# The sample's input projections with the tokens as the stationary operand and the weight panels streaming

## The chip, the cores and the metric

The kernel runs on one core of a Trainium2 chip. The metric is the device time of one execution in microseconds. The core's engines are TensorE (PE in the profile, with its weight loads as PEld), VectorE (DVE), ScalarE (ACT), GpSimd (POOL) and SyncE (SP), whose queue issues the DMAs.

## What is computed

Two layers of a hybrid decoder. A layer normalises its input, multiplies it by one wide matrix `w_in` (1024 x 3920), and gives the slices of the product to four recurrent mixers side by side: retention, HGRN2, GLA and RWKV-7. Their gated outputs go through `w_out`, and a cross-attention to 256 memory tokens follows.

```python
h = rmsnorm(x, norm_mix[l])
p_ret, p_hgrn, p_gla, p_rwkv = split(h @ w_in[l])      # the input projections
o_ret  = retention(rotary(q), rotary(k), v) * silu(g)
o_hgrn = gated_linear(silu(q), (1 - lb) * sigmoid(-f), v=i, log_f) * silu(g)
o_gla  = gated_linear(q, k, v, log_a) * silu(g)
o_rwkv = rwkv7(p + (previous_row - p) * mu) * silu(g)
x = x + concat(o_ret, o_hgrn, o_gla, o_rwkv) @ w_out[l]
x = x + cross_attend(rmsnorm(x, norm_x[l]), memory)
```

This is done for a prompt of 2048 tokens and, with the same weights, for a sample of 8 sequences of 8 tokens each (64 rows), which starts from given states.

## The kernel before

The prompt goes through in four blocks of 512 tokens per layer, so there are eight steps `(l, b)`. The sample's 64 rows ride along: their input projections are made in block 0 of the layer, next to the prompt's, because the weights are there; the four gates' projections for the sample are made in block 1 (`TURN`). The mixers of the sample run as chains of their own: RWKV and GLA in block 0, HGRN and retention in block 1.

Weights come in panels. `load_c` loads a panel of 128 output channels, `load_t` one of 256 in two halves. In block 0 a raw fp32 panel (`wraw`, pool `wrp`, 3 buffers of each) is loaded and `split_w` makes two fp32r parts of it (`whl`, pool `whp`, 3 buffers): the high part by a copy on ScalarE (line 358), the low part by a subtraction on GpSimd. The two parts are stored to DRAM and later blocks load them from there. With `plain` set, `parts_of` gives back the raw panel too, and loads it even where the parts come from DRAM; this is so for the sample's gates in block 1.

The prompt's products use three terms, high x high, high x low and low x high, in fp32r. `dense_c` has the panel's parts stationary and 512 tokens streaming, so channels come out as rows; `dense_t` has 128 tokens stationary and 256 channels streaming, so tokens come out as rows. The sample's products use the raw panel and the raw tokens `hts` (128 x 8 x 64) in plain fp32. `dense_cs` has 64 columns of the panel stationary and the 64 tokens streaming, two halves of the panel into two halves of the PSUM bank. `dense_ts` does the same for a panel of 256 channels, so its result has channels as rows, though the mixer wants tokens as rows: `totok` transposes it later, in the mixer's part of the program (GLA's and HGRN's values, retention's query, key and value).

A layer has 21 column projections for the sample (one of 80 channels for the low-rank inputs, six for RWKV's r, k and v, two for GLA, four for HGRN, eight gates) and 5 row projections.

All these products write PSUM tiles of pool `psd`, which has two banks (`PS("d")`); the mixers' products use the pools `psa`, `psc` and `psb`. A product's bank comes free once it has been read out: for the sample by `shift_mix_s` (RWKV), by copies, by `silu2` (HGRN's query) or in the gates by `evs`.

The order of instructions on each engine is fixed when the program is built, by a list scheduler with priorities: program order, shifted by `PRI` under the name that `rank` gives, and raised for runs of matmuls (`held`). A tile of a tag with one buffer (pool `dnp`, where the projections' results lie) can be written only after the last reader of the tile that had the buffer before. A mixer's working tiles are in pools that are opened one after the other (`wk1` RWKV's prompt part, `wk1s` RWKV's sample, `wk5` GLA's sample, and so on).

Of the kernel before, what the change touches and what calls it, by code (L numbers as in the profile page):

```python
# [142 lines left out]
def decoder(ctx, tc, I, C, O):  # L143
# [270 lines left out]
    def dense_cs(w, hts, ps):  # L414
        raw, hl, M = w
        for k in range(8):
            for h in range(0, M, 64):
                e = min(M, h + 64)
                mm(ps[h:e, :SN], raw[:, k, h:e], hts[:, k, :], k == 0, k == 7)
# [5 lines left out]
    def dense_ts(w, hts, c, ps):  # L425

        for k in range(8):
            for h in (0, 64):
                mm(ps[h:h + 64, :SN], w[k // 4][0][:, k % 4, c * 128 + h:c * 128 + h + 64], hts[:, k, :], k == 0, k == 7)
# [39 lines left out]
    def norm_sample(xt, gcol, hts, wp, xs):  # L469
# [801 lines left out]
    def block(l, b, act, hts, st, smp, on, ons, ds, op):  # L1271
# [15 lines left out]
        wt = load_c([(col("rw_w", 0, 32), 0), (col("rw_a", 0, 32), 32), (col("gla_l", 0, 16), 64)], (l, "low"), smp, not final)  # L1287
# [4 lines left out]
        if smp:  # L1292
            sms = T("sms", [128, SN])
            G.memset(sms[64:128], 0.0)
            ps = PS("d")
            dense_cs(wt, hts, ps)
            shift_mix_s(ps[:80, :SN], 0, c, st["shs"], st["ssh"], sms[:80], 80)
            A.activation(sms[0:32], sms[0:32], AF.Tanh)
        rk = {}
        rks = {}  # L1300
        for j, nm in enumerate("rkv"):
            x = T("dn_" + nm, [128, 2, TB], tag="dn4", bufs=8)
            xs = T("ds_" + nm, [128, 2, SN], tag="ds_" + nm) if smp else None
            for i in range(2):
                wt = load_c([(col("rw_" + nm, i * 128), 0)], (l, "rw", nm, i), smp, not final)
                ps = PS("d")
                dense_c(wt, act, ps)
                shift_mix(ps, 1 + 2 * j + i, c, carry, x[:, i, :])
                if smp:
                    ps = PS("d")  # L1310
                    dense_cs(wt, hts, ps)
                    shift_mix_s(ps[:, :SN], 1 + 2 * j + i, c, st["shs"], st["ssh"], xs[:, i, :])
            rk[nm] = x
            rks[nm] = xs
# [5 lines left out]
        def proj_t(nm, ev, evs):  # L1320
            wt = load_t(col(nm, 0, 256), (l, nm), smp, again=not final)
            for t0 in (0, 2):
                ps = PS("d").rearrange("p (t n) -> p t n", t=2)
                for t in range(2):
                    dense_t(wt, act, t0 + t, ps[:, t, :])
                ev(ps, t0)
            if smp:
                ps = PS("d")
                for i in range(2):
                    dense_ts(wt, hts, i, ps[:, i * SN:])  # L1330
                copy_ps(evs, ps[:, :2 * SN].rearrange("p (c n) -> p c n", c=2))

        def proj_c(nm, o, ev, evs, smp=smp, hts=hts):
            wt = load_c([(col(nm, o), 0)], (l, nm, o), smp, not final)
            ps = PS("d")
            dense_c(wt, act, ps)
            ev(ps)
            if smp:
                ps = PS("d")
                dense_cs(wt, hts, ps)  # L1340
                evs(ps[:, :SN])
# [32 lines left out]
        qks = T("ds_qk", [128, 2, SN]) if smp else None  # L1374
# [4 lines left out]
        gvs = T("ds_gv", [128, 2, SN]) if smp else None  # L1379
# [7 lines left out]
        if b == TURN["gla"]:  # L1387
            with left("wk5") as wp:
                x = ds["gla"]
                R_gla(l, sa, None, dict(x, v=totok(x["v"], 2, sa, wp, "sv", 256)), ons["gla"], wp)  # L1390
        if b == TURN["hgrn"]:
            with left("wk6") as wp:
                x = ds["hgrn"]
                R_hgrn(l, sa, None, dict(x, v=totok(x["v"], 2, sa, wp, "sv", 256)), ons["hgrn"], wp)
        if b == TURN["ret"]:
            with left("wk7") as wp:
                x = {nm: totok(ds["ret"][nm], 2, sa, wp, "sv" + nm, 256) for nm in "qkv"}
# [35 lines left out]
        rqs = {nm: T("ds_r" + nm, [128, 2, SN]) if smp else None for nm in "qkv"}  # L1433
# [360 lines left out]
    def pre_norm(l, b, wp, out, start=False):  # L1794
# [226 lines left out]
```

## Time and profile before

| | us |
|---|---|
| median of 3 runs (lowest to highest) | 3630.43 (3629.65 to 3630.89) |
| the profiled execution | 3625.24 |
| its span | 3623.4 |
| TensorE busy | 3419.7 (94%) |
| TensorE weight loads busy | 2842.5 (78%) |
| VectorE busy | 2283.1 (63%) |
| ScalarE busy | 1393.4 (38%) |
| GpSimd busy | 562.1 (16%) |

Busy time is the time in which at least one instruction of the engine is recorded as running. Matmuls are pipelined, so that records of successive matmuls overlap; what one costs in a stream is read from the distance between starts. A product in plain fp32 leaves two records, one in fp32r leaves one; both are labelled f32. In a tile's name the part before `<-` is what is written, the part behind it the streaming and the stationary operand. The chain of waits is followed back from the last instruction.

### The profile page before, as it was taken

To read this page: it belongs to the slowest core of one execution; us is meant where nothing else is said; L and a number is where in the kernel's file an instruction comes from. 1 tells how busy PE (TensorE), PEld (TensorE's weight loads), DVE (VectorE), ACT (ScalarE), POOL (GpSimd) and SP (SyncE) were. 2 spreads that over 40 slices of the span, in tenths; PEclk is the share of its full clock that TensorE was granted. 3 is DMA by queue.
4 is the path that set the end of the run, shared out by engine and by line. 5 is a ranking of instruction groups with operands and counts; after the bars stand their busy time and mean duration, and the time that the engine had idled before them with its cause. 6 is when DMAs were issued, how large, how long until landed. Compare 5 with 4: busy or idle time off the path is not lost.

```text
span 3623.4 us, 87919 instructions
## 1 busy us (share of the span) xinstructions
PE 3419.7 (94%) x35978; PEld 2842.5 (78%) x35978; DVE 2283.1 (63%) x7543; ACT 1393.4 (38%) x3489; POOL 562.1 (16%) x760
## 2 busy tenths in 40 slices
PE   7899999999999999999999898999989999999998
PEld 5767887778887887788877777778778878877887
DVE  4677645776347754776468765468644577547754
ACT  4443344513235324532445423553214442254323
POOL 3323331020000100110122233101200001000100
PEclk9998999999999999999999989999889999999999
DMA  6432674236652254225442247531555522542254
GB/s 189 150 106 83 214 232 170 72 108 215 210 178 94 92 188 152 105 76 185 164 163 89 98 135 256 176 130 69 151 169 178 180 76 97 200 167 91 72 195 186
DMA packets 244152, 530.87 MB, mean 147 GB/s; under 512 B 66982, under 2 KB 181926, under 8 KB 199718
## 3 DMA queue, kind: packets, MB, share of 16 engines
q1 hardware_dynamic: 243750, 525.25, 42.7%
q8 instruction: 284, 4.65, 0.5%
q14 instruction: 118, 0.97, 0.1%
HBM read 410.04 MB, written 115.16 MB: 145 GB/s over the span
## 4 chain that ended last, share of the span: by engine, by line
PE 73%; DVE 14%; ACT 5%; issue 4%; DMA 2%; POOL 1%; SPq 0%; POOLq 0%; ACTq 0%; DVEq 0%
PE psd L230 39%; PE psc L230 12%; PE psa L230 11%; PE psb L230 5%; PE psc L272 2%; PE psa L272 2%; PE psb L272 2%; DVE rsq L236 1%; DVE Wb L936 1%; DMA wraw<-in_w_in 1%; POOL whl L236 1%; ACT Xb L938 1%; DVE hss L561 1%; DVE sT L745 0%; DVE osb L236 0%
## 5 line engine op out<-in xcount | busy, mean ns | idle before, releaser
L230 PE MATMUL psd<-act,whl 128*128 128x512 f32 (+1 forms) x4032 | 1014.9, 404 | 24.8 <-DVE th L1265 12.9
L230 PEld LDWEIGHTS psd<-act,whl 128*128 128x128 f32 (+1 forms) x4032 | 751.7, 191 | 200.3 <-DVE th L1265 14.7
L230 PE MATMUL psd<-whl,act 128*128 128x256 f32 x3840 | 550.9, 295 | 6.3 <-POOL whl L236 4.6
L230 PEld LDWEIGHTS psd<-whl,act 128*128 128x128 f32 x3840 | 492.3, 196 | 28.6 <-issue 10.3
L236 POOL TENSOR_TENSOR whl<-wraw,whl 128x1024 fp32r<-128x1024 f32 (+1 forms) x90 | 217.7, 2422 | 333.5 <-ACT whl L358 328.5
L230 PE MATMUL psd<-whl,oh 128*128 128x256 f32 x1152 | 211.6, 284 | 2.1 <-DMA whl<-w_w_out 1.5
L280 POOL TENSOR_TENSOR ri<-ri,mhalf 128x1 f32<-128x1 f32 (+1 forms) x87 | 50.0, 575 | 1048.3 <-DVE ri L279 1041.4
L230 PEld LDWEIGHTS psd<-whl,oh 128*128 128x128 f32 x1152 | 177.6, 189 | 3.3 <-DMA whl<-w_w_out 1.7
L230 PE MATMUL psd<-whl,ol 128*128 128x256 f32 x576 | 162.9, 283 | 0.0
L938 ACT ACTIVATE Xb<-X 32x128 f32<-32x128 f32 x324 | 99.1, 306 | 126.1 <-DVE X L954 78.7
L358 ACT ACTIVATE whl<-wraw 128x1024 fp32r<-128x1024 f32 (+1 forms) x90 | 94.1, 1048 | 128.2 <-PE psa L230 40.7
L745 DVE COPY_PREDICATED sT<-upack,psb 128x128 f32<-128x128 uint8 x320 | 92.5, 326 | 41.7 <-PE psb L230 38.2
L236 DVE TENSOR_TENSOR x<-x,psd 128x256 f32<-128x256 f32 x72 | 30.3, 421 | 128.6 <-PE psd L230 128.6
L230 PEld LDWEIGHTS psd<-whl,ol 128*128 128x128 f32 x576 | 108.6, 189 | 0.4 <-DVE ol L236 0.4
L230 PE MATMUL psb<-dn_hq,dn_hf 64*64 64x32 f32 (+1 forms) x3840 | 101.5, 226 | 7.2 <-DVE dn_hq L236 3.2
L230 PEld LDWEIGHTS psb<-dn_hq,dn_hf 64*64 64x64 f32 x3840 | 83.8, 139 | 31.3 <-issue 17.8
L435 ACT ACTIVATE xs<-xn 128x1024 f32<-128x1024 f32 (+1 forms) x34 | 35.9, 1054 | 153.2 <-PE psb L272 150.0
L1265 DVE SCALAR_TENSOR_TENSOR th<-th,psd 128x512 f32<-128x512 f32 x48 | 32.6, 686 | 90.5 <-ACT th L1264 90.4
L230 PE MATMUL psd<-hts,wraw 128*64 128x64 f32 x1984 | 83.9, 229 | 1.9 <-DVE th L1265 1.9
L230 PEld LDWEIGHTS psd<-hts,wraw 128*64 128x64 f32 x1984 | 69.9, 140 | 20.0 <-issue 10.5
L230 PE MATMUL psa<-whl,oh 128*128 128x256 f32 x448 | 82.8, 283 | 0.0
L230 PE MATMUL psc<-whl,oh 128*128 128x256 f32 x448 | 82.7, 283 | 0.0
(760 smaller groups left out, 7361.1 us busy)
## 6 DMA issues: line engine op xcount, KB each, us to landing
whl<-w_w_out SPq DMA_DIRECT2D x56, 1024.0 KB
wraw<-in_w_in SPq DMA_DIRECT2D x76, 512.0 KB
wraw<-in_w_out SPq DMA_DIRECT2D x32, 512.0 KB
w_w_out<-whl SPq DMA_DIRECT2D x16, 1024.0 KB
x<-x SPq DMA_DIRECT2D x32, 512.0 KB
whl<-w_rw_r SPq DMA_DIRECT2D x12, 1024.0 KB
whl<-w_rw_k SPq DMA_DIRECT2D x12, 1024.0 KB
whl<-w_rw_v SPq DMA_DIRECT2D x12, 1024.0 KB
```

Of the source, the lines that this page charges most:

```text
L230: PE.matmul(out, lhsT=lhsT, rhs=rhs, start=start, stop=stop, skip_group_check=True)
L236: e.tensor_tensor(out, a, b, op)
L272: PE.transpose(out, in_, ident[:rows, :rows])
L280: G.tensor_tensor(y, y, mhalf[:P], ALU.pow)
L358: A.activation(hl[:, 0], raw, AF.Copy)
L435: A.activation(out, xt, AF.Square, accum_out=ss[:P])
L561: V.tensor_reduce(ss[:P, :n4], sq[:P, :n4], AX.X, ALU.add)
L745: V.copy_predicated(out, bc(mk, [P, w, 32 // s, s]), ps)
L936: V.tensor_copy(o, i)
L938: A.activation(o, i, AF.Copy)
L1265: V.scalar_tensor_tensor(th, th, 1.0, x, ALU.add, ALU.mult)
```

## The change

For the sample, the normed tokens `hts` become a tile of 128 x 8 x 128 fp32r: the high parts of the 64 tokens beside their low parts. They are the stationary operand, and the panel's two fp32r parts stream past them. A column projection is 16 matmuls (8 slices of the contraction x 2 parts) into a bank with 128 rows, tokens by high and low; ScalarE copies it to SBUF (`scs`, in the buffer of `ths`), and one fp32 matmul against `I64` (two stacked identities) adds the two halves and turns the result into channel rows. A row projection is 16 matmuls of 256 channels, a copy of the upper half and an addition of the lower half, and leaves the tokens as rows, so `totok` is not called for it. No sample projection reads the raw panel any more (`plain` is False). Several of the sample's result tiles share buffers: `ds0` to `ds2` are RWKV's r, k, v and then retention's q, k, v; `ds3` is GLA's value and then HGRN's; `ds4` is GLA's query and key and then HGRN's query.

```diff
-    def dense_cs(w, hts, ps):
-        raw, hl, M = w
-        for k in range(8):
-            for h in range(0, M, 64):
-                e = min(M, h + 64)
-                mm(ps[h:e, :SN], raw[:, k, h:e], hts[:, k, :], k == 0, k == 7)
+    def dense_cs(w, hts):
+
+        _, hl, M = w
+        ps = PS("d")
+        group(ps[:, :M], [(hts[:, k, :], hl[:, j, k, :M]) for k in range(8) for j in range(2)])
+        x = dnp.tile([128, 128], F32, name="scs", tag="ths")
+        A.activation(x[:, :M], ps[:, :M], AF.Copy)
+        ps = PS("d")
+        mm(ps[:M, :SN], x[:, :M], K["I64"])
+        return ps[:M, :SN]
...
-    def dense_ts(w, hts, c, ps):
-
-        for k in range(8):
-            for h in (0, 64):
-                mm(ps[h:h + 64, :SN], w[k // 4][0][:, k % 4, c * 128 + h:c * 128 + h + 64], hts[:, k, :], k == 0, k == 7)
+    def dense_ts(w, hts, out):
+
+        ps = PS("d")[:, :256]
+        group(ps, [(hts[:, k, :], w[k // 4][1][:, j, k % 4, :]) for k in range(8) for j in range(2)])
+        A.activation(out[:SN, 0], ps[:SN], AF.Copy)
+        tt(V, out[:SN, 0], out[:SN, 0], ps[SN:2 * SN], ALU.add)
...
-        tt(V, hts, ps, bc(gcol[:, 0:8].unsqueeze(2), [128, 8, SN]), ALU.mult)
+        x = xs[:, 0:8 * SN].rearrange("p (k n) -> p k n", k=8) if parts else out
+        tt(V, x, ps, bc(gcol[:, 0:8].unsqueeze(2), [128, 8, SN]), ALU.mult)
+        if parts:
+            A.activation(out[:, :, :SN], x, AF.Copy)
+            tt(V, out[:, :, SN:], x, out[:, :, :SN].bitcast(F32), ALU.subtract)
...
-            wt = load_c([(col(nm, o), 0)], (l, nm, o), smp, not final)
+            wt = load_c([(col(nm, o), 0)], (l, nm, o), False, not final)
             ps = PS("d")
             dense_c(wt, act, ps)
             ev(ps)
             if smp:
-                ps = PS("d")
-                dense_cs(wt, hts, ps)
-                evs(ps[:, :SN])
+                evs(dense_cs(wt, hts))
...
-        qks = T("ds_qk", [128, 2, SN]) if smp else None
+        qks = T("ds_qk", [128, 2, SN], tag="ds4") if smp else None
...
-        gvs = T("ds_gv", [128, 2, SN]) if smp else None
+        gvs = T("ds_gv", [128, 1, 256], tag="ds3") if smp else None
...
-                R_gla(l, sa, None, dict(x, v=totok(x["v"], 2, sa, wp, "sv", 256)), ons["gla"], wp)
+                R_gla(l, sa, None, x, ons["gla"], wp)
...
-        hqs = T("ds_hq", [128, 2, SN]) if smp else None
+        hqs = T("ds_hq", [128, 2, SN], tag="ds4") if smp else None
         hfs = T("ds_hf", [128, 2, SN]) if smp else None
-        hvs = T("ds_hv", [128, 2, SN]) if smp else None
+        hvs = T("ds_hv", [128, 1, 256], tag="ds3") if smp else None
...
-        rqs = {nm: T("ds_r" + nm, [128, 2, SN]) if smp else None for nm in "qkv"}
+        rqs = {nm: T("ds_r" + nm, [128, 1, 256], tag="ds%d" % j) if smp else None for j, nm in enumerate("qkv")}
...
-            hts = stp.tile([128, 8, SN], F32, name="hts", tag="hts")
+            hts = stp.tile([128, 8, 2 * SN], F32R, name="hts", tag="hts")
             x = load(xsrc_s(l), SN)
-            norm_sample(x[:SN], cols[l]["g_mix"], hts, wp, scratch())
+            norm_sample(x[:SN], cols[l]["g_mix"], hts, wp, scratch(), True)
```

The RWKV projections, the low-rank ones and HGRN's and retention's mixers are changed in the same way.

## Rows read from the trace of the kernel before

**Rows 1.** The page's first lines: span, and TensorE's busy time.

```profile
span 3623.4 us, 87919 instructions
PE 3419.7 (94%) x35978; PEld 2842.5 (78%) x35978; DVE 2283.1 (63%) x7543; ACT 1393.4 (38%) x3489; POOL 562.1 (16%) x760
```

**Rows 2.** Busy time of the engines, summed over eight stretches with sample projections.

```profile
sum 939.00, PE 855.51 PEld 689.81 DVE 626.07 ACT 364.51 POOL 233.37; mean PE 106.94 PEld 86.23 DVE 78.26 ACT 45.56 POOL 29.17
```

**Rows 3.** TensorE's timeline (start, length, engine, what): sample projections, columns then rows.

```profile
1974.99 1.15 PE L230 MATMUL psd<-hts,wraw 128*64 128x64 f32 x32
1976.07 3.03 PE L230 MATMUL psd<-act,whl 128*128 128x512 f32 x12
...
2151.85 2.08 PE L230 MATMUL psd<-hts,wraw 128*64 128x64 f32 x64
```

**Rows 4.** TensorE's timeline: fp32r runs of 512 and 256 columns, then plain fp32.

```profile
3102.64 11.16 PE L230 MATMUL psd<-act,whl 128*128 128x512 f32 x48
3113.63 0.41 PE L230 MATMUL psd<-whl,oh 128*128 128x256 f32 x2
...
91.39 7.31 PE L230 MATMUL psd<-whl,mh 128*128 128x256 f32 x60 [0.89 <-ACT ds_v L542]
98.53 0.60 PE L272 MATMUL psc<-fpack,wk_xs 128*128 128x128 f32 x4
...
1963.32 0.61 PE L230 MATMUL psc<-vl,w 128*128 128x128 f32 x4
1963.77 0.38 PE L272 MATMUL psa<-fpack,dn_v 128*128 128x128 f32 x2
```

**Rows 5.** Timeline of weight loads, then the products: retention's outputs.

```profile
406.47 0.53 PEld L230 LDWEIGHTS psc<-dn_rv,sT 128*128 128x128 f32 x4
406.92 0.30 PEld L230 LDWEIGHTS psc<-S_ret,rqT 128*128 128x128 f32 x2
...
406.58 0.56 PE L230 MATMUL psc<-dn_rv,sT 128*128 128x64 f32 x4
```

**Rows 6.** Groups by line (busy us, mean ns, idle before): a 128x128 copy from PSUM.

```profile
L944 ACT ACTIVATE XB<-psc 128x128 f32<-128x128 f32 x80 | 22.0, 275 | 15.3 <-PE psc L272 14.3
```

**Rows 7.** Timeline of all engines in the second block's gates, first layer.

```profile
874.82 1.15 PE L230 MATMUL psd<-hts,wraw 128*64 128x64 f32 x32
...
876.35 5.76 PE L230 MATMUL psd<-act,whl 128*128 128x512 f32 x24 [0.38 <-DVE th L1265]
...
877.13 0.63 ACT L1463 ACTIVATE oh<-th 128x512 fp32r<-128x512 f32 x1 [0.89 <-DVE th L1266]
```

**Rows 8.** The chain of waits (start, length): loads of raw panels behind sample projections.

```profile
63.71 6.06 DMA wraw<-in_w_in
...
256.06 4.69 DMA wraw<-in_w_in
...
1896.92 3.94 DMA wraw<-in_w_in
...
1959.91 3.86 DMA wraw<-in_w_in
```

**Rows 9.** VectorE's timeline: HGRN's sample query written, GLA's read last, both layers.

```profile
248.71 0.22 DVE L533 SCALAR_TENSOR_TENSOR ds_hq<-th,psd 128x64 f32<-128x64 f32 x1
...
380.65 0.69 DVE L236 TENSOR_TENSOR qx<-ds_qk,s_bmask 128x512 f32<-128x512 f32 x1
...
1993.33 0.22 DVE L533 SCALAR_TENSOR_TENSOR ds_hq<-th,psd 128x64 f32<-128x64 f32 x1
...
2126.58 0.69 DVE L236 TENSOR_TENSOR qx<-ds_qk,s_bmask 128x512 f32<-128x512 f32 x1
```

**Rows 10.** Groups by line, 258.0 to 381.4 us, then 2005.0 to 2127.3 us.

```profile
L230 PE MATMUL psd<-whl,act 128*128 128x256 f32 x311 | 48.9, 309 | 1.6 <-POOL whl L236 1.3
...
L230 PE MATMUL psd<-whl,act 128*128 128x256 f32 x321 | 48.6, 301 | 3.4 <-POOL whl L236 3.3
```

**Rows 11.** The page's chain that ended last: shares of the span by engine.

```profile
PE 73%; DVE 14%; ACT 5%; issue 4%; DMA 2%; POOL 1%; SPq 0%; POOLq 0%; ACTq 0%; DVEq 0%
```

More of the change, by code (lines that the diff above doesn't have):

```diff
@@ L467, in scaled_tr, with norm_sample @@
                 tt(V, a[:, 1, :, sl], xg, a[:, 0, :, sl].bitcast(F32), ALU.subtract)
-    def norm_sample(xt, gcol, hts, wp, xs):
+    def norm_sample(xt, gcol, out, wp, xs, parts=False):
         norm_rows(xt, SN, wp, xs[:SN])
@@ L1286, in block @@
         G.memset(sm[64:128], 0.0)
-        wt = load_c([(col("rw_w", 0, 32), 0), (col("rw_a", 0, 32), 32), (col("gla_l", 0, 16), 64)], (l, "low"), smp, not final)
+        wt = load_c([(col("rw_w", 0, 32), 0), (col("rw_a", 0, 32), 32), (col("gla_l", 0, 16), 64)], (l, "low"), False, not final)
         ps = PS("d")
@@ L1294, in block @@
             G.memset(sms[64:128], 0.0)
-            ps = PS("d")
-            dense_cs(wt, hts, ps)
-            shift_mix_s(ps[:80, :SN], 0, c, st["shs"], st["ssh"], sms[:80], 80)
+            ps = dense_cs(wt, hts)
+            shift_mix_s(ps, 0, c, st["shs"], st["ssh"], sms[:80], 80)
             A.activation(sms[0:32], sms[0:32], AF.Tanh)
@@ L1302, in block @@
             x = T("dn_" + nm, [128, 2, TB], tag="dn4", bufs=8)
-            xs = T("ds_" + nm, [128, 2, SN], tag="ds_" + nm) if smp else None
+            xs = T("ds_" + nm, [128, 2, SN], tag="ds%d" % j) if smp else None
             for i in range(2):
-                wt = load_c([(col("rw_" + nm, i * 128), 0)], (l, "rw", nm, i), smp, not final)
+                wt = load_c([(col("rw_" + nm, i * 128), 0)], (l, "rw", nm, i), False, not final)
                 ps = PS("d")
@@ L1309, in block @@
                 if smp:
-                    ps = PS("d")
-                    dense_cs(wt, hts, ps)
-                    shift_mix_s(ps[:, :SN], 1 + 2 * j + i, c, st["shs"], st["ssh"], xs[:, i, :])
+                    ps = dense_cs(wt, hts)
+                    shift_mix_s(ps, 1 + 2 * j + i, c, st["shs"], st["ssh"], xs[:, i, :])
             rk[nm] = x
@@ L1320, in proj_t @@
         def proj_t(nm, ev, evs):
-            wt = load_t(col(nm, 0, 256), (l, nm), smp, again=not final)
+            wt = load_t(col(nm, 0, 256), (l, nm), False, again=not final)
             for t0 in (0, 2):
@@ L1327, in proj_t @@
             if smp:
[L1328 to L1331, printed above, removed]
+                dense_ts(wt, hts, evs)
         def proj_c(nm, o, ev, evs, smp=smp, hts=hts):
-            wt = load_c([(col(nm, o), 0)], (l, nm, o), smp, not final)
+            wt = load_c([(col(nm, o), 0)], (l, nm, o), False, not final)
             ps = PS("d")
@@ L1338, in proj_c @@
             if smp:
-                ps = PS("d")
-                dense_cs(wt, hts, ps)
-                evs(ps[:, :SN])
+                evs(dense_cs(wt, hts))
         rank("R_vf")
@@ L1393, in block @@
                 x = ds["hgrn"]
-                R_hgrn(l, sa, None, dict(x, v=totok(x["v"], 2, sa, wp, "sv", 256)), ons["hgrn"], wp)
+                R_hgrn(l, sa, None, x, ons["hgrn"], wp)
         if b == TURN["ret"]:
             with left("wk7") as wp:
-                x = {nm: totok(ds["ret"][nm], 2, sa, wp, "sv" + nm, 256) for nm in "qkv"}
+                x = dict(ds["ret"])
                 tab = sample_const("rots", wp).unsqueeze(1)
```

## The prediction

> **What bounds the kernel now.** I read the page's first section before anything else: TensorE has work in flight for 3419.7 of 3623.4 us, 94% of the span [rows 1]. The next most busy engine, VectorE, has 63%. So a microsecond of TensorE time added or taken away anywhere is, to a first reading, a microsecond of the whole, and the question is where the sample's projections stand. They are in eight stretches: the first block of either layer, and the gates of the second block. The busy time by stretch (the second view) says that TensorE is busy there for 855.5 of 939.0 us, 91% [rows 2]: nearly full, with 83.5 us of gaps. The third view is TensorE's timeline, for what one projection costs. A column projection of the sample (21 in a layer, 42 in all) is 32 records, 16 calls of two records each, and the next instruction starts 1.08 us after its first [rows 3]. A row projection (5 in a layer, 10 in all) is 64 records; with the 0.07 us by which records overlap it holds the engine for 2.01 us [rows 3]. All of them together are 42 x 1.08 + 10 x 2.01 = 65.5 us, 1.8% of the span. That is all that the change could take away on TensorE, if the new form cost nothing.
>
> The profiled execution took 3625.24 us, its span 3623.4; the median of the runs is 3630.43, 0.14% above. I make the sum as a difference and put it on the median.
>
> **What the new form costs on TensorE.** A column projection becomes 16 calls on fp32r operands, which leave one record each: a stationary operand of 128 columns (64 tokens, high parts beside low parts) and 128 moving columns, one panel part each. No row of the trace shows an fp32r product with fewer than 256 moving columns. The bounds: at 512 columns one takes (3113.63 - 3102.64)/48 = 0.229 us, at 256 columns (98.53 - 91.39)/60 = 0.119 us [rows 4]. The slope is 0.110 us for 256 columns, so if the stream alone counted, 128 columns would take 0.119 - 0.055 = 0.064 us: the lower end. But every call loads its stationary operand anew, even where it is that of the call before. The nearest row for a 128-column load with a short stream is the retention output's: stationary 128 columns, 64 moving, and its loads follow each other at (406.92 - 406.47)/4 = 0.112 us [rows 5], though 64 columns stream in at most half of the 0.112 us that 128 take [rows 4]. So I take the load as the pace, between 0.112 and 0.119 us: 0.116. The upper end, if a short fp32r stream ran like a plain fp32 one, is two records of (1963.77 - 1963.32)/4 = 0.112 us [rows 4], 0.225 us a call.
>
> At 0.116 the 16 calls take 1.86 us. Behind them comes the turn back into channel rows, a product of 128 stationary and 64 moving columns in plain fp32: two records at the load's pace, 0.22 us [rows 5]. Together 2.08 us for 1.08: **+1.00 us, x 42 = +42.0 us**. A row projection becomes 16 calls of 256 moving columns: 16 x 0.119 = 1.90 for 2.01, **x 10 = -1.1 us**. The ten turns into token rows (totok) go away, two transposes of 128 columns at 0.112 each [rows 4]: **x 10 = -2.2 us**.
>
> The Trainium skill speaks both for and against this. TensorEngine Tiling, Key Properties, says that a change of the tiling mode drains the engine, and the old form does change it, from 128-column to 64-column tiles and back; such a drain already lies within the 1.08 us measured, so the sum would stay as it is. TensorE: Matmul & The Clock Gate, section Back-to-back issue gap, gives some 81 ns for a load and a product of 128 columns in a steady stream. By it the 16 calls would take 1.30 us, and the 42 projections +18 instead of +42; the fp32 loads of this trace at 0.112 disagree, but no row shows fp32r ones.
>
> **The round trip.** The turn back has to wait for ScalarE to copy the product out of PSUM, 0.28 us by the copy of a 128x128 tile [rows 6]. Where other work for TensorE is at hand this costs nothing. In the second block's gates there is none: dense projections stand one behind the other, and two PSUM banks (pool psd) serve them. There the next dense product starts 876.35 - 874.82 = 1.53 us after the sample's first record [rows 7]. After the change it is 1.86 + 0.55 (the last product in flight, 0.61 - 3 x 0.112 = 0.27 by [rows 4], and the copy) + 0.22 = 2.6 us, +1.1 instead of +1.00; ScalarE can be some 0.6 later still, since a 0.63 us copy for the output projection stands in its queue at that point [rows 7]. I take +0.2 for each of 16 gates: **+3 us**. The 42 copies themselves (12 us of ScalarE) and ten adds on VectorE lie beside other work. The high and low parts of the normed tokens cost two operations in a layer; I count nothing.
>
> **What it gives back.** The raw panel is read by nobody but the split any more, so its buffer is free before the sample's product and not after it. In the chain of waits four loads of a raw panel start right behind a sample projection, 6.06, 4.69, 3.94 and 3.86 us, 18.6 us in all [rows 8]. TensorE was mostly at work during them, so I take a quarter: **-5 us** (bounds 0 and -18.6). The gates of the second block load sixteen raw panels of 512 KB fewer; no wait on a DMA stands in the rows there, so this counts nothing. Of the added work some falls into the 9% of gaps [rows 2]: **-4 us**. Subtotal: 42.0 - 1.1 - 2.2 + 3 - 5 - 4 = **+33 us**.
>
> **The new wait.** The sample's tiles now share buffers, and one pair collides. HGRN's query takes the buffer of GLA's query and key (ds4), its value that of GLA's value (ds3). In the kernel before HGRN's query is written at 248.71 us and GLA's tile is last read by the operation that starts at 380.65; in the second layer 1993.33 and 2126.58 [rows 9]. So the write must move behind the read, by 132 us, unless the GLA sample comes earlier, and that stands behind the RWKV mixers' work. The product that waits to be written holds a PSUM bank of psd; the second HGRN query projection comes to hold the other. Then no dense product can start until GLA's sample is through, and these are what TensorE does between the mixers' short steps: 311 products of 256 columns in that stretch of the first layer, 321 in the second [rows 10], at 0.119 each 37 and 38 us. Queued behind the wait are HGRN's value, which HGRN's outputs need, and retention's query, key and value. Against the whole loss speaks that the mixers, without dense groups in between, come through sooner. I know no row that says by how much, so the bounds are 0 and 37 us a layer, and I take the middle, 18: **+36 us**. The sum is 33 + 36 = +69 us: **3699 us**.
>
> **The rivals.**
> Wait swallowed: the mixers speed up by as much as is deferred, or the order of work avoids the collision. The sum is +33: 3663 us. For it: 94% busy means that mixers and dense work now compete.
> Stream as pace: loads of fp32r hide behind the stream. 16 x 0.064 + 0.22 - 1.08 = +0.16 us a projection, +7 instead of +42: 3664 with the wait, 3628 without it, which would be no change. Against it: the loads of rows 5.
> Short streams at fp32's price: 16 x 0.225 + 0.22 - 1.08 = +2.74 us a projection, +115 instead of +42: 3772 us. For it only that every fp32r product of this kernel has 256 columns or more, so that no row excludes it.
> Faster: not TensorE but the chain through the weight buffers sets the first blocks. Then the added products fall into the 83.5 us of gaps [rows 2], the four loads' 18.6 us [rows 8] come back, and there is no new wait: 3612 us. It decides once the gaps at those places are longer than the added 1.0 us. The chain of waits gives DMA 2% of the span and TensorE 73%, which speaks against it [rows 11].
>
> **How the numbers follow.** Forecast as summed 0.55, wait swallowed 0.15, stream as pace with the wait 0.08 and without it 0.05, fp32's price 0.09, faster 0.08. The forecast's own range: up to 16 x 0.119 + 0.22 - 1.08 = 1.04 a projection (+44), 37 us a layer (+74), nothing given back, 44 - 3 + 3 + 74 = +118: 3748 us; down to the swallowed wait's 3663 less what more of the loads' 18.6 us may give, 3650. The stream's case without the wait puts the lower end at 3628; outside 3628 to 3748 stand fp32's price and the faster case, 0.17 together. A measurement of this kernel can tell about 0.2% from no change. Slower by more than that has 0.55 + 0.15 + 0.08 + 0.09 = 0.87, within 0.2% 0.05, faster 0.08.
>
> **What would show it.** In the profile after: the sample's column products at 0.11 to 0.12 us each (0.06 or 0.22 would be the rivals); 2.1 us of TensorE for each of 42 projections; the write of HGRN's sample query after GLA's last read, and in the 100 us before it few products of 256 columns on psd, with gaps on TensorE; in the gates 8.2 to 8.4 us from one dense product to the next for 7.2; the raw panels' loads gone from the second block's gates. The forecast is wrong if the dense products run on through that stretch, or if the mixers' end comes earlier by as much as they are deferred.

## The result and the profile after

The changed kernel takes 3782.61 us, the kernel before 3630.04 beside it: a ratio of 1.0435, interval 1.0416 to 1.0455, +153 us. The forecast had the direction and both causes, but 3699 us, and its range ended at 3748.

The page of the changed kernel: span, TensorE's busy time, and the granted clock in 40 slices.

```profile
span 3781.4 us, 85822 instructions
PE 3509.7 (93%) x34890; PEld 2922.3 (77%) x34890; DVE 2313.7 (61%) x7555; ACT 1401.8 (37%) x3523; POOL 556.2 (15%) x760
...
PEclk9986999999999999999999689999869999999999
```

TensorE is busy for 90.0 us more than in [rows 1], with 1088 records fewer, and idle for 271.7 us in place of 203.7. Where: the last product of the output projection stands at 516.8, 950.0, 1368.8, 1764.4, 2275.9, 2741.8, 3161.8 and 3565.0 us in the eight steps before, and at 569.1, 1012.0, 1432.1, 1826.1, 2401.4, 2888.9, 3313.5 and 3722.6 after. The steps grew by 52, 10, 1, -2, 64, 22, 5 and 6 us. So 116 us lie in the two first blocks, where the projections of the sample are made, and 31 in the two blocks with its gates.

TensorE's timeline after (start, length, engine, what), a column projection and its turn back, against [rows 3]:

```profile
45.79 1.90 PE L230 MATMUL psd<-whl,hts 128*128 128x128 f32 x16
47.52 0.63 PE L272 MATMUL psa<-fpack,xs 128*128 128x128 f32 x4
48.17 0.41 PE L230 MATMUL psd<-fpack,scs 128*128 128x64 f32 x2
48.39 0.96 PE L230 MATMUL psd<-act,whl 128*128 128x512 f32 x3
```

VectorE's timeline after, against [rows 9]: the last reads of GLA's query and key and the writes of HGRN's sample query, first layer and then second.

```profile
352.37 0.71 DVE L236 TENSOR_TENSOR qx<-ds_qk,s_bmask 128x512 f32<-128x512 f32 x1
...
353.23 0.25 DVE L542 SCALAR_TENSOR_TENSOR ds_hq<-th,psd 128x64 f32<-128x64 f32 x1
...
2184.04 0.71 DVE L236 TENSOR_TENSOR qx<-ds_qk,s_bmask 128x512 f32<-128x512 f32 x1
...
2184.90 0.25 DVE L542 SCALAR_TENSOR_TENSOR ds_hq<-th,psd 128x64 f32<-128x64 f32 x1
```

The write has moved from 248.71 to 353.23 us and from 1993.33 to 2184.90, right behind the last read. What TensorE does in the meantime is in the groups by line from 258 to 353.2 us, first layer (the group, count, busy time, mean ns, idle before). First all groups of the kernel after that read a weight panel:

```profile
L230 PE MATMUL psd<-act,whl 128*128 128x512 f32 x24 | 6.0, 399 | 0.0
L230 PE MATMUL psd<-whl,hts 128*128 128x128 f32 x22 | 3.2, 281 | 0.0
```

and the same stretch of the kernel before:

```profile
L230 PE MATMUL psd<-whl,act 128*128 128x256 f32 x216 | 34.0, 309 | 1.5 <-POOL whl L236 1.3
L230 PE MATMUL psd<-hts,wraw 128*64 128x64 f32 x128 | 4.8, 226 | 0.0
```

The 216 dense products of 256 columns (of the 311 of [rows 10]) have become none; the next one on psd starts at 361.91 us. The stretch by engines, after (busy time and count of each, the granted clock, DMA):

```profile
258.00:353.20 95.20, 68.83 (x848) 48.82 (x847) 54.16 (x209) 30.60 (x84) 22.23 (x29) 0.67 0.19 54
```

and before:

```profile
258.00:353.20 95.20, 88.45 (x1340) 70.87 (x1339) 72.35 (x239) 32.54 (x86) 31.08 (x35) 0.88 0.27 93
```

TensorE idles for 26 us in place of 7, and its granted clock is 0.67 in place of 0.88; from 300 to 350 us it is 0.50, the lower of its two levels, 1.2 GHz.

### The profile page after: what moved, and what is told of

It reads as the page before. It is cut to its first block, busy times and chain, and to the rows that moved or that the text cites. A ratio compares the mean times of both kernels' runs of the same rounds, so it can differ in the third digit from the quotient of the medians.

```text
span 3781.4 us, 85822 instructions
## 1 busy us (share of the span) xinstructions
PE 3509.7 (93%) x34890; PEld 2922.3 (77%) x34890; DVE 2313.7 (61%) x7555; ACT 1401.8 (37%) x3523; POOL 556.2 (15%) x760
## 4 chain that ended last, share of the span: by engine, by line
PE 73%; DVE 15%; ACT 6%; issue 3%; DMA 2%; POOL 1%; SPq 0%; ACTq 0%; POOLq 0%; DVEq 0%
PE psd L230 39%; PE psa L230 12%; PE psc L230 11%; PE psb L230 5%; PE psc L272 2%; PE psb L272 2%; PE psa L272 2%; DVE rsq L236 1%; ACT Xb L947 1%; DVE Wb L945 1%; DVE hss L570 1%; DVE hri L292 1%; DMA whl<-w_low 1%; DVE dn_hq L236 1%; DVE qx L236 0%
## 5 line engine op out<-in xcount | busy, mean ns | idle before, releaser
L230 PE MATMUL psd<-act,whl 128*128 128x512 f32 (+1 forms) x4032 | 1040.2, 411 | 4.3 <-DMA whl<-w_low 2.0
L230 PEld LDWEIGHTS psd<-act,whl 128*128 128x128 f32 (+1 forms) x4032 | 765.9, 195 | 182.0 <-issue 9.0
L230 PE MATMUL psd<-whl,act 128*128 128x256 f32 x3840 | 537.6, 292 | 0.9 <-POOL whl L236 0.6
L230 PEld LDWEIGHTS psd<-whl,act 128*128 128x128 f32 x3840 | 484.7, 194 | 21.0 <-issue 9.8
L230 PE MATMUL psd<-whl,hts 128*128 128x128 f32 (+2 forms) x832 | 112.4, 284 | 4.3 <-DVE th L1274 3.4
L230 PEld LDWEIGHTS psd<-whl,hts 128*128 128x128 f32 x832 | 105.2, 196 | 11.4 <-DVE th L1274 4.0
L757 POOL MEMSET sT<- 64x512 f32 x32 | 16.8, 523 | 493.6 <-ACT sT L756 368.4
L945 DVE COPY Xb<-X 32x128 f32<-32x128 f32 x324 | 79.6, 247 | 7.7
```

What stands on the lines that cost most here:

```text
L945: V.tensor_copy(o, i)
```

## The experiments

Each time stands beside the kernel before on the same chip; differences are against that.

| run | edit | us | before | ratio (interval) |
|---|---|---|---|---|
| e1 | before, query and value share | 3703.21 | 3621.91 | 1.0221 (1.0205 to 1.0238) |
| e9 | before, query alone shares | 3703.13 | 3623.95 | 1.0221 (1.0195 to 1.0247) |
| e10 | before, value alone shares | 3624.76 | 3623.95 | 1.0002 (0.9985 to 1.0018) |
| e12 | before, ds0 to ds2 alone shared | 3622.47 | 3623.95 | 1.0004 (0.9989 to 1.0020) |
| g1 | before, all shared, query staged | 3627.08 | 3628.12 | 0.9996 (0.9985 to 1.0008) |
| e2 | before, hts twice as wide | 3784.22 | 3621.91 | 1.0444 (1.0428 to 1.0460) |
| e6 | before, query and value share, hts wide | 3711.36 | 3623.16 | 1.0247 (1.0221 to 1.0272) |
| e5 | before, two raw buffers | 3680.80 | 3623.16 | 1.0161 (1.0133 to 1.0189) |
| e3 | after, two raw buffers | 3788.93 | 3621.91 | 1.0459 (1.0435 to 1.0484) |
| e4 | e3, own buffers for HGRN's query and value | 3739.97 | 3621.91 | 1.0317 (1.0298 to 1.0335) |
| f1 | after, own buffer for the query | 4127.75 | 3624.02 | 1.1384 (1.1363 to 1.1405) |
| e11 | after, no turn back | 3749.12 | 3623.95 | 1.0341 (1.0319 to 1.0363) |
| e7 | e4, gates' turns in psc | 3744.26 | 3623.16 | 1.0337 (1.0313 to 1.0361) |
| e8 | e4, all turns in psc | 3848.75 | 3623.16 | 1.0625 (1.0590 to 1.0660) |
| f2 | after, late gates' turns in psc | 3778.70 | 3624.02 | 1.0429 (1.0412 to 1.0447) |
| f3 | before, late sample gates in psc | 3615.08 | 3624.02 | 0.9978 (0.9966 to 0.9989) |
| f4 | before, late prompt gates in psc | 3598.35 | 3624.02 | 0.9926 (0.9911 to 0.9941) |
| g2 | f3 and f4 | 3599.19 | 3628.12 | 0.9918 (0.9898 to 0.9938) |

### Shared buffers or room on the chip

The trace after had shown a second oddity: HGRN's mixer for the prompt started at 338.90 us in place of 274.70, just when RWKV's sample was through. So there were two theories: the shared buffers (T), and the wider hts that leaves less SBUF (the working memory on the chip, counted in bytes for each partition) for the mixers' pools (M). e1 has the first alone:

```diff
-        gvs = T("ds_gv", [128, 2, SN]) if smp else None
+        gvs = T("ds_gv", [128, 2, SN], tag="ds3") if smp else None
...
-        hqs = T("ds_hq", [128, 2, SN]) if smp else None
+        hqs = T("ds_hq", [128, 2, SN], tag="ds4") if smp else None
```

(and the same for qks and hvs.)

> The kernel before with one part of the change alone: HGRN's sample query takes the buffer of GLA's (ds4), HGRN's sample value that of GLA's value (ds3). No product is changed. Theory T (the shared buffers make the loss): HGRN's sample query is written behind the last read of ds_qk, psd's products of 256 columns thin out in the stretch before it, and the time rises by 152 - 33 = about 119 us, at least 80: 3710 to 3750 us. Theory M (the doubled hts leaves less SBUF and pushes HGRN's mixer for the prompt behind RWKV's sample): no memory is taken here, so 3630 to 3650. Both: in between, 3660 to 3710. My prediction's term for this wait was +36: 3666.

e2 has the second alone:

```diff
-            hts = stp.tile([128, 8, SN], F32, name="hts", tag="hts")
+            hts = stp.tile([128, 8, 2 * SN], F32, name="hts", tag="hts")[:, :, :SN]
```

> The kernel before with hts allocated twice as wide (2 KB more for each partition), its second half not used; nothing else is changed, no instruction added or taken away. Theory M: HGRN's mixer for the prompt starts only when RWKV's sample is through, about 339 us in place of 275, and the time rises by 80 to 119: 3710 to 3750 us. Theory T: within 20 us of the kernel before, 3630 to 3650.

Both cost: e1 +81 us, e2 +162. Neither theory had that. e2 has every instruction that it had before, and HGRN's mixer for the prompt starts at 461.4 us in place of 274.70 (VectorE's groups for the tile ha, e2):

```profile
L828 DVE TENSOR_SCALAR ha<-dn_hf,c,c x2: 408/409/410, 461.4 to 461.8; 128x256 f32<-128x256 f32 x2
```

From 500 to 550 us TensorE is then busy for 27.68 of 50 us (the stretch by engines, e2), since this mixer comes when little dense work is left:

```profile
500.00:550.00 50.00, 27.68 (x435) 24.86 (x432) 28.51 (x87) 10.99 (x22) 3.87 (x9) 0.62 0.05 17
```

That 2 KB for each partition do this is shown, since nothing else was changed; that the mixer's pool then comes to lie on buffers of other mixers is argued from it. The changed kernel, however, frees room by sharing. So e6 puts both edits together, which gives the kernel before nearly the buffers of the kernel after:

> The kernel before with both things that cost alone, the shared ds3 and ds4 and the doubled hts, so with nearly the buffers of the kernel after, but with the old products. If the two losses add up: 3622 + 81 + 162 = 3865. If the shared buffers make room for the doubled tile again, or one wait lies inside the other: 3700 to 3790. Against the kernel after (3783): if this lies at 3680 or less, the products cost 100 or more in the kernel after; if it lies at 3750 or more, they cost at most 33, as in my sum.

They don't add up: e6 is +88 us, 7 to 9 over e1 (by the difference of the times or of the ratios), which the intervals hardly tell apart. HGRN's mixer starts at 340.7 us, as in the kernel after. So room on the chip took little of the 153 us, though it came near to a cliff. What is left between e6 and the kernel after, 1.0435 - 1.0247, some 68 us, is the new form of the products (ds0 to ds2, which e6 doesn't share, cost nothing in e12 below).

Two runs of the changed kernel with more room look at the split from the other side. HGRN's query and value get buffers of their own there, for which the raw panels have two buffers instead of three; e3 has the two raw buffers alone:

```diff
-    wrp = ctx.enter_context(pool("wrp", 3))
+    wrp = ctx.enter_context(pool("wrp", 2))
```

> The kernel after with two buffers instead of three for the raw panels (pool wrp), which frees SBUF; the shared buffers ds3 and ds4 stay. Theory T: HGRN's sample query still waits for GLA's sample, so at least 3740 us, up to 3790. Theory M: HGRN's mixer starts where it did before, and the time comes down to 3663 to 3690. Both: 3690 to 3740.

e4 gives HGRN's query and value buffers of their own besides.

```diff
-        hqs = T("ds_hq", [128, 2, SN], tag="ds4") if smp else None
+        hqs = T("ds_hq", [128, 2, SN]) if smp else None
...
-        hvs = T("ds_hv", [128, 1, 256], tag="ds3") if smp else None
+        hvs = T("ds_hv", [128, 1, 256]) if smp else None
```

> The kernel after with own buffers for HGRN's sample query and value, and two instead of three for the raw panels, without which they don't fit. What is left is the new form of the products. By my sum without the new wait 3663 us, bounds 3645 to 3690 (two raw buffers may cost some). Theory T: HGRN's query is written long before GLA's last read, and this lies at least 60 us below the kernel after with two raw buffers alone. Theory M: it lies within 20 us of that one. A third theory, that the products themselves and the turn back cost the 152 us where they stand: still 3750 or more.

e5 is the control for both, the kernel before with two raw buffers.

> The kernel before with two buffers instead of three for the raw panels and nothing else changed: the control for the two kernels that needed this to have room. If the third buffer does nothing: within 10 us of the kernel before (3612 to 3632 beside 3622), and the kernel after with own buffers, 3740, owes its whole loss of 118 to the new form of the products. If the third buffer carries the load of the next panel: 3650 to 3700, and the products cost that much less; my sum of +33 for them would ask for about 3707.

e3 is +167 us, e4 +118, e5 +58. With two raw buffers the shared buffers are worth 167 - 118 = 49 us, against the 79 that e1 and e9 show in the kernel before. What is left for the products hangs on the third raw buffer. If it is worth in the changed kernel the 58 us that e5 shows in the kernel before, they cost 118 - 58 = 60 us. But e3 lies only 1.0459 - 1.0435, some 9 us, above the changed kernel, third buffer and room taken together (HGRN's mixer starts at 282.5 us in e3 for 338.90); if 9 us is all that it is worth there, the products cost 118 - 9 = 109. The price of the shared buffers and that of the products depend on what else is in the kernel; these runs do not settle the split, and e6 gives it only along its own path.

f1 was to take the shared query back in the changed kernel itself, with three raw buffers: the first half of e4's diff (and two constants of one column in one tile, to make it fit).

> The kernel after with an own buffer for HGRN's sample query; the value and the other tiles stay shared, three raw buffers as there. If the shared query buffer costs in the kernel after what it costs alone in the kernel before: 3783 - 79 = about 3704, between 3690 and 3720. If memory is what counts here (half a KB more for each partition where 2 KB more were taken already, as in the kernel with doubled hts and own buffers, which lost 162): 3750 to 3800, and HGRN's mixer for the prompt starts later than the 339 us of the kernel after.

It fell over the cliff of e2: +504 us, HGRN's mixer at 458.1 us, and the steps that have no sample grew too. It says nothing on the query's buffer, only what half a KB more can cost where SBUF is nearly full.

### Which shared buffer, and what it costs by

e9 has of e1's edit the query's half alone:

```diff
-        qks = T("ds_qk", [128, 2, SN]) if smp else None
+        qks = T("ds_qk", [128, 2, SN], tag="ds4") if smp else None
...
-        hqs = T("ds_hq", [128, 2, SN]) if smp else None
+        hqs = T("ds_hq", [128, 2, SN], tag="ds4") if smp else None
```

> The kernel before with ds4 alone shared: HGRN's sample query in GLA's sample query's buffer; the values keep their own. The query has two products (two panels), so two waiting products can hold both banks of psd. Theory of the held banks: as with both shared buffers, 3622 + 81 = about 3700, between 3685 and 3710. If it is the value's wait that costs (its readers come later in GLA's sample): 3625 to 3650.

e10 has the value's half (gvs and hvs with the tag ds3):

> The kernel before with ds3 alone shared: HGRN's sample value in that of GLA's. One product waits, from about 296 us to GLA's last read of its value at 358. Theory of the held banks: it holds one bank; the next group takes the other and its own results have their buffers, but the two banks are used in turn, so that the group behind it stops too: a hold of some 60 us a layer instead of 110, 3640 to 3680. If one bank is enough to go on: 3620 to 3635.

e12 has the other three shared buffers alone:

```diff
-            xs = T("ds_" + nm, [128, 2, SN], tag="ds_" + nm) if smp else None
+            xs = T("ds_" + nm, [128, 2, SN], tag="ds%d" % j) if smp else None
...
-        rqs = {nm: T("ds_r" + nm, [128, 2, SN]) if smp else None for nm in "qkv"}
+        rqs = {nm: T("ds_r" + nm, [128, 2, SN], tag="ds%d" % j) if smp else None for j, nm in enumerate("qkv")}
```

> The kernel before with ds0 to ds2 shared alone (RWKV's r, k and v, then retention's q, k and v), which frees 1.5 KB of each partition and whose new writer comes after the old reader anyway (retention's query at about 311 us, RWKV's sample done at about 310 to 338). Theory of the held banks: no bank is held for long, so within 10 us of the kernel before, 3612 to 3632; if the room that it frees lets a mixer start earlier, below that, to 3590. If any shared buffer in this list costs by its order alone: 3650 or more.

The query alone costs all of it (e9, +79 us); the value (e10) and ds0 to ds2 (e12) cost nothing that can be told. In e9 the query is written at 357.44 us, right behind GLA's last read, as in the kernel after (VectorE's timeline, e9):

```profile
356.64 0.69 DVE L236 TENSOR_TENSOR qx<-ds_qk,s_bmask 128x512 f32<-128x512 f32 x1 [1.34 <-DMA s_bmask<-c_bmask]
357.44 0.35 DVE L533 SCALAR_TENSOR_TENSOR ds_hq<-th,psd 128x64 f32<-128x64 f32 x2
```

The page of e9 (its TensorE line):

```profile
PE 3446.7 (93%) x35978; PEld 2859.9 (77%) x35978; DVE 2273.7 (61%) x7543; ACT 1393.7 (38%) x3489; POOL 558.4 (15%) x760
```

The same 35978 records as in [rows 1] hold TensorE for 27.0 us more, and the rest of the longer span (3698.8 less 3623.4), 48.4 us, is idle time. In the first layer no product on psd starts between these two, the end of the second query's sample product and the next dense one (TensorE's timeline, e9):

```profile
264.51 0.45 PE L230 MATMUL psd<-hts,wraw 128*64 128x64 f32 x8
...
365.16 2.07 PE L230 MATMUL psd<-whl,act 128*128 128x256 f32 x8
```

A stretch inside by engines, e9:

```profile
300.00:350.00 50.00, 38.32 (x346) 23.33 (x346) 26.45 (x96) 14.27 (x41) 12.82 (x14) 0.50 0.06 13
```

and before:

```profile
300.00:350.00 50.00, 45.32 (x524) 34.46 (x523) 41.05 (x111) 16.61 (x44) 24.76 (x23) 0.81 0.36 124
```

While the query waits, TensorE gets little work, and the granted clock falls to 0.50 for 0.81 in the kernel before. That fits both numbers, but doesn't show yet what starves TensorE: the two banks that the waiting products hold, or the wait and the order that it forces on GLA's sample. g1 keeps the wait and frees the banks. The query is made in a tile of its own, and copied into the shared one later; ds0 to ds4 are all shared, which makes the room.

```diff
-                proj_c("hg_q", i * 128, lambda ps: silu2(ps, hq[:, i, :], TB, gp), lambda ps: silu2(ps, hqs[:, i, :], SN, gp))
+                proj_c("hg_q", i * 128, lambda ps: silu2(ps, hq[:, i, :], TB, gp), lambda ps: silu2(ps, hqx[:, i, :], SN, gp))
+        if smp:
+            A.activation(hqs, hqx, AF.Copy)
```

> The kernel before with the change's shared buffers ds0 to ds4, HGRN's query in GLA's buffer among them, but HGRN's sample query is first made in a tile of its own, which frees the bank of psd at once, and ScalarE copies it into the shared buffer once GLA's sample is through. The wait for the shared buffer stays, the held banks go. Theory of the held banks: the dense products run on, 3618 to 3635. If the wait itself, or what is scheduled earlier for it, is the cost: 3690 to 3705 as with the shared query alone.

3627.08 us, ratio 0.9996 (0.9985 to 1.0008): the cost is gone, the wait is still there. The query is written to its own tile from 246.9 us on, and the copy waits for GLA's last read, which starts at 374.94 (ScalarE's timeline, g1):

```profile
375.66 0.31 ACT L1425 ACTIVATE ds_hq<-ds_hx 128x128 f32<-128x128 f32 x1 [0.79 <-DVE qx L236]
```

and the dense products beside it (g1's groups by line, 258 to 381.4 us; 311 in [rows 10]):

```profile
L230 PE MATMUL psd<-whl,act 128*128 128x256 f32 x288 | 44.6, 306 | 2.5 <-ACT whl L358 1.7 <-POOL whl L236 0.9
```

So the held banks are the cause of the query's 79 us. The Trainium skill, PSUM — Partial Sum Buffer, section Summary: rules for kernel authors, says that PSUM should be evacuated promptly; g1 and e9 put a price on that rule here, 79 us for two tiles in each layer that are not.

### What the products cost beyond TensorE's own work

The changed kernel against e6, both with nearly the same buffers: by their pages TensorE is busy for 3509.7 and 3466.2 us, +43.5, of a longer span of 3781.4 - 3714.6 = 66.8; the other 23.3 us are idle time. e11 leaves the copy and the turn back out:

```diff
-        x = dnp.tile([128, 128], F32, name="scs", tag="ths")
-        A.activation(x[:, :M], ps[:, :M], AF.Copy)
-        ps = PS("d")
-        mm(ps[:M, :SN], x[:, :M], K["I64"])
         return ps[:M, :SN]
```

> The kernel after without the copy of a column product to SBUF and without the turn back into channel rows: what reads the result takes it from the first product's bank (this leaves out that part of the computation). The 42 column projections keep their 16 products. If the round trip costs what my sum says, TensorE's 0.22 us for each of 42 and 3 us in the gates: 3783 - 9 - 3 = about 3770. If the round trip is what the products cost beyond my sum (the kernel after lies 71 us above the kernel before with the same buffers, for 33): 3783 - 12 - 38 = about 3733, between 3720 and 3750.

1.0435 - 1.0341, some 34 us, go with it (29.4 by the two profiled spans); I had 12 for it. By the pages TensorE is busy for 3489.2 us in e11, so 20.5 of the 29.4 us are its busy time and 8.9 idle time. What is left of e11 over e6, 1.0341 - 1.0247, again some 34 us, stands against the 42 x (1.86 - 1.08) - 1.1 - 2.2 = 29.5 us that my sum has for the sixteen products and the rows. The changed kernel's groups by line, whole span, the second idle number being the releaser's share:

```profile
L230 PE MATMUL psd<-whl,hts 128*128 128x128 f32 x640 | 85.9, 283 | 4.2 <-DVE th L1274 3.4 <-DVE dn_hq L542 0.8
L230 PE MATMUL psd<-whl,hts 128*128 128x256 f32 x160 | 22.4, 288 | 0.0
L230 PE MATMUL psd<-fpack,scs 128*128 128x64 f32 x80 | 20.1, 340 | 15.7 <-ACT scs L420 12.4 <-DVE ssm L1496 3.2
...
L230 PE MATMUL psd<-fpack,scs 128*80 128x64 f32 x4 | 0.7, 259 | 1.8 <-ACT scs L420 1.8
```

The turns back are in flight for 20.8 us, where I had 42 x 0.22 = 9.2, and TensorE stands 17.5 us ahead of them, mostly for ScalarE's copy; 11.5 of these lie in the two first blocks, 5.9 in the gates' blocks. In the second block's gates it looks like this (all engines, after, from the timeline):

```profile
938.97 1.90 PE L230 MATMUL psd<-whl,hts 128*128 128x128 f32 x16
...
941.25 0.63 ACT L1465 ACTIVATE oh<-th 128x512 fp32r<-128x512 f32 x1 [1.48 <-DVE th L1275]
...
941.79 0.26 ACT L420 ACTIVATE scs<-psd 128x128 f32<-128x128 f32 x1
942.10 0.30 PEld L230 LDWEIGHTS psd<-fpack,scs 128*128 128x128 f32 x2 [1.37 <-ACT scs L420]
942.10 0.43 PE L230 MATMUL psd<-fpack,scs 128*128 128x64 f32 x2 [1.23 <-ACT scs L420]
```

The products end at 940.87. ScalarE could copy then, but in its queue the copy stands behind the prompt's gate (oh<-th), which waits for VectorE until 941.25. The next dense product starts 942.34 - 938.97 = 3.37 us after the sample's first, for 1.53 in [rows 7].

Is it the bank? e7 gives the turn a bank of psc in all gates of the second block (on e4), e8 for all 42 projections:

```diff
-        ps = PS("d")
+        ps = psc.tile([128, 512], F32, name="psc", tag="c") if own else PS("d")
         mm(ps[:M, :SN], x[:, :M], K["I64"])
```

> The kernel after with own buffers and two raw buffers, and the turn back of the second block's gates into a bank of psc, a pool that is free there, instead of psd. In that kernel a gate lasts 9.0 to 10.5 us for 7.2 before: TensorE stands 1.2 us behind each sample product until ScalarE, which stands behind the prompt's gate, has copied it, and the next dense product has no bank. Theory of the bank: the next dense product runs during the copy, a gate lasts 8.2 to 8.5 us, 16 gates by about 1.2: 20 us less than 3740, so 3715 to 3725. If the copy is not what TensorE waits for: 3735 to 3745.

> The same, with the turn back in a bank of psc for all 42 column projections, the first blocks' too. If the round trip through psd also costs there, and the 26 of them lose 1 to 2 us each: another 25 to 50 us less than the kernel with the gates alone, 3670 to 3695. If they cost only TensorE's time for loads and streams there: the same as the gates alone, 3715 to 3725. If the mixers' products, to which psc belongs, are in the way: more than 3725, and the turns stand late in TensorE's order.

In e7 the stall is gone, as the theory has it: the next dense product runs while ScalarE copies, and the turn back stands in the middle of it (TensorE's timeline, e7):

```profile
907.53 3.03 PE L230 MATMUL psd<-act,whl 128*128 128x512 f32 x12 [0.16 <-DVE th L1274]
910.39 0.33 PE L230 MATMUL psc<-fpack,scs 128*128 128x64 f32 x2
910.54 2.97 PE L230 MATMUL psd<-act,whl 128*128 128x512 f32 x12
913.35 0.89 PE L230 MATMUL psd<-whl,hts 128*128 128x128 f32 x7
```

The last six sample gates start 7.6 us apart, the last five in e4 9.6. The time did not follow: 3744 for 3740 us. Two sample gates start ahead of 900 us where e4 has three; the others moved behind the mixers, and TensorE is busy for 40.84 us from 850 to 900 in place of 45.44. e8 is worse by 100 us; no sample product starts there from 244.9 to 356.6 us, and psc is the mixers' pool. I followed it no further. f2 moves the turns of the last four gates of the second blocks in the changed kernel, and leaves the early ones in psd:

> The kernel after with the turn back of the last four gates of the second block (HGRN's and retention's) in a bank of psc; the first four, which run beside the mixers, stay in psd. If the wait for a bank is what a gate loses beyond TensorE's own work: 8 gates by 1.5 to 2 us, 12 to 16 us less, 3767 to 3771. If the gates' order is what counts: 3780 to 3790, as with all gates moved, which gave nothing.

1.0429 for 1.0435: no gain that can be told. So the gates' stall is seen in the trace, and a bank removes it in e7, but it doesn't set the time of the block there. The turn back's cost lies elsewhere: against the kernel after, the steps of e11 are shorter by 8 and 16.5 us in the two first blocks and by 0 and 2.5 in the gates' blocks. In the two first blocks TensorE's busy time is shorter by 8.8 and 9.7 us: in the first layer that is all of the gain, in the second some 7 us are idle time. Why the turns take more busy time than their 9.2 us is not settled.

### A faster kernel

[rows 7] show that the kernel before has a stall at the same place: TensorE stands 0.38 us ahead of the dense product, for VectorE's read of the prompt's gate, which I take for the wait for a bank. f3 puts the sample's product of the last four gates into psc, f4 every second prompt gate of HGRN and retention, in all steps (f4's edit; f3's and f2's have the same form, with own set for the names hg_g and ret_g in f2):

```diff
-            ps = PS("d")
+            ps = psc.tile([128, 512], F32, name="psc", tag="c") if nm in ("hg_g", "ret_g") and o else PS("d")
             dense_c(wt, act, ps)
```

> The kernel before with the sample's product of HGRN's and retention's gates (8 in all) in a bank of psc instead of psd. There TensorE stands 0.4 to 0.5 us ahead of the next dense product at each of these gates, with VectorE's read of the prompt's gate as the releaser. If that is the bank: 8 x 0.45 = 3.6 us less, 3618 to 3621 beside 3623, at the edge of what can be told. If not: 3623.

> The kernel before with every second of HGRN's and retention's gates for the prompt in a bank of psc, in all eight steps (16 gates). If the two banks hold TensorE between gates: 16 times 0.4 to 0.5 us less, 3612 to 3618 beside 3623. If the mixers' products, which use psc, move: 3623 or more.

> The kernel before with every second of HGRN's and retention's prompt gates and all of their sample gates in a bank of psc. If the two gains (26 and 9 us) add up: 3589. If the sample's product in psc takes the bank that the prompt's gate wants there: 3598 to 3610.

f3 is 0.22% faster, f4 0.74%, both together 0.82% (0.62 to 1.02 by the interval); whether the two gains add up, to 0.96%, can't be told from that. The groups by line of the kernel before (the dense products of 512 columns):

```profile
L230 PE MATMUL psd<-act,whl 128*128 128x512 f32 (+1 forms) x4032 | 1014.9, 404 | 24.8 <-DVE th L1265 12.9 <-DVE carry L539 7.5 <-DVE act L236 2.3
```

and of f4:

```profile
L230 PE MATMUL psd<-act,whl 128*128 128x512 f32 (+1 forms) x3648 | 921.4, 404 | 14.1 <-DVE carry L539 6.5 <-DVE act L236 2.4 <-DVE th L1265 1.2
...
L230 PE MATMUL psc<-act,whl 128*128 128x512 f32 x384 | 95.1, 402 | 1.0 <-DMA whl<-w_hg_g 1.0
```

The wait for the gate's bank has gone from 12.9 to 1.2 us. That is less than half of the 26 us gained; where the rest came from I didn't follow. All three are faster than both kernels of this case.

## Why the prediction was wrong, step by step

**The products' price was right.** A column projection goes at 0.112 us a call, the middle distance between starts of its products and of its loads where the granted clock is near 1.0 (1.90 us for sixteen, the last in flight included); I had 0.116. The rivals with the stream as the pace and with fp32's price are out. The rule of the Trainium skill's page TensorE: Matmul & The Clock Gate, section Back-to-back issue gap, 81 ns for 128 columns, is not met by this trace: it has 112. The sum of the products, +42.0 - 1.1 - 2.2 = 38.7 us, stands against 43.5 us more of busy time between e6 and the kernel after.

**The round trip was mis-sized.** I wrote that it costs nothing where other work is at hand, and 3 us in the gates. e11 makes it 34 us with TensorE's own part, for 12 in my sum. In the gates I had seen the 0.63 us copy that stands ahead in ScalarE's queue, and took 0.2 us for it; it waits for VectorE in turn, and the sample's products start 8.9 to 10.5 us apart there (from 930.04 us on), where I had 8.2 to 8.4. But taking that stall away gained nothing (f2). The first blocks, where I took the round trip as covered, carry most of the loss, and the greater part of it is TensorE's busy time and not waiting.

**What it gives back was half right.** The raw panels' loads fell from 76 to 60, and the first layer's seven early projections run from 36.98 to 86.39 us, 49.4 in place of 54.3 (35.05 to 89.34): 5 us less there although the products cost more. No run has this term alone. The -4 us that gaps were to take up are not: TensorE's idle time grew by 23.3 us with the products. The gaps of [rows 2] were not free places; that they are the mixers' steps, and that a product with a wait of its own makes new ones, is my reading and not shown.

**The new wait was the right mechanism at less than half its size.** That the query's write moves behind GLA's last read, that both banks of psd are held, and that no dense product runs meanwhile came out as written, and g1 shows that the banks are the cost. The step that failed is "I take the middle": 18 us a layer, on the ground that the mixers come through sooner without dense work. They do: GLA's last read comes at 356.64 us in e9 for 380.65 in [rows 9]. But in e9 the first block of the first layer grew by 49 us, of the second by 33 (by the last product of the output projection). The first is over my upper bound of 37, which counted the deferred products at the price they have at full clock. From 13.5 us to the last output product of that block (566.2 us in e9, 516.8 before), TensorE is busy for 481.75 us in e9 in place of 462.64, at a granted clock of 0.88 in place of 0.94, and idle for 71.0 in place of 40.7. So 19 of the 49 us are the same work in more busy time, at a lower granted clock, and 30 are gaps. I had priced neither. The value's wait, which I named with the query's, costs nothing that can be told (e10).

**One term was missing.** The wider hts stands nowhere in the sum. It did little beside the shared buffers (e6 against e1), which make room for it; alone it costs 162 us (e2), as much as the whole change.

With 79 us for the query's buffer, some 9 for the room and some 68 for the products the sum is 156 for the 153 measured. That is one path from the kernel before to the kernel after, so the three add up by their making; with two raw buffers the shared buffers cost 49. The range's upper end failed because it let one bound go to its end, 74 us for the wait, which took 79, and kept 3 us for the round trip, which had no bound at all.

## What to carry to other kernels

A PSUM bank of this kernel is held until its last reader has run (e9), so ask of each shared SBUF buffer not only when it comes free but which bank waits for it; with two banks, two waiting tiles stop a whole stream of products, and a small staging tile takes the cost away (g1). Price a second pass through PSUM by leaving it out of the kernel, as e11 does: the waits that are easiest to see, ahead of its copy in the gates, were not what it cost. Where pools fill SBUF, treat half a KB or 2 KB for each partition as a change of its own (f1, e2), and give each experiment that frees room its control.

## What the runs showed that I had not expected

The granted clock was lower where the dense products were missing: with nothing but the mixers' short products on TensorE it stood at 0.50 from 300 to 350 us in e9 and in the kernel after, for 0.81 in the kernel before, though TensorE was busy for 38.32 of the 50 us in e9. A third buffer of 4 KB for the raw panels is worth 58 us in the kernel before (e5), and 2 KB that nobody reads cost 162 (e2).
